# A decoder trunk in split fp32: the gates' first product on paired token factors, weight sums begun a step earlier, and loads issued by the blocks in use

## The chip, the core and the metric

The kernel runs on one core of a Trainium2 chip. A core has five engines with a queue of instructions each: TensorE (PE in the profile; its weight loads are PEld), VectorE (DVE), ScalarE (ACT), GpSimd (POOL) and SyncE (SP, which here only issues transfers). Sixteen DMA engines carry the transfers that SP and POOL issue. The metric is the device time of one execution in microseconds (us), the median of several runs.

## The reference

Two layers over 512 tokens of 1024 features, all in fp32: a gated short convolution with a gated feed-forward behind it, then windowed attention with 16 heads and a gated feed-forward again. The feed-forwards hold most of the work: `w_gate_up` is 1024 x 5632, `w_down` 2816 x 1024.

```python
D_MODEL, BATCH, SEQ, DEPTH = 1024, 1, 512, 2
D_FF = ((8 * D_MODEL // 3 + 255) // 256) * 256          # 2816

def swiglu(h, w_gate_up, w_down):
    g, u = jnp.split(h @ w_gate_up, 2, axis=-1)
    return (jax.nn.silu(g) * u) @ w_down

def reference(x, ...):
    h = x
    for l in range(DEPTH):
        if l < N_A:
            mix = short_conv_mixer(rmsnorm(h, a_pre_norm[l]), a_w_in[l], a_conv_w[l], a_w_out[l])
            h = h + rmsnorm(mix, a_post_norm[l])
        else:
            ...
            attn = sliding_window_sink_attention(q, k_sh, v_sh, b_sinks[j]) @ b_w_o[j]
            h = h + rmsnorm(attn, b_post_norm[j])
        ff = swiglu(rmsnorm(h, ffn_pre_norm[l]), ffn_w_gate_up[l], ffn_w_down[l])
        h = h + rmsnorm(ff, ffn_post_norm[l])
    return h
```

## The kernel before

**Split numbers.** Every factor of a product is split into a high part (`whi`, `xhi`: a copy by ScalarE in the type that TensorE multiplies fast) and a low part (`wlo`, `xlo`: the rest, by a subtraction on VectorE), and `mm3` (L190 to L193) multiplies three times: high by low, high by high, low by high.

**Seven products.** The gates (`gate_jobs`, L976) work on one *quarter* at a time: a stretch of `w_gate_up` for 256 gate features and their 256 up features, in ten quarters a layer, 20 in all. Weights and tokens are cut in two halves each way, and a quarter is computed by seven products of half size instead of eight, in the order 1, 2, 6, 5, 7, 3, 4. Each product takes sums of weight blocks (`a11`, `a21`, `s1`, ...) and sums of token tiles. Products 1, 2 and 3 take token tiles as they are (`xhi`, `xlo`: product 1 the first four of eight, 2 and 3 the last four). For products 4 to 7, `factors` (L364) makes sums of tiles, and lays high and low part of each side by side in one wide buffer (`xt`), so that `factors[p][k][2]` is a right-hand side of 512 columns, 256 high and 256 low.

Products 1, 6, 7 and 4 go into the same two banks (`gx`, chain "X"). In `run` (L1032), a product with such a pair and chain "X" is *wide*: eight matmuls of 128x512 multiply the high weights by high and low tokens at once (L1047), the low tokens' sum landing in the bank's second half, and eight of 128x256 add low weights by high tokens to the first half (L1050). All other products use `mm3`: 24 matmuls of 128x256. What is read after a product is in `take` (L1001): ScalarE copies the first half of a bank into `st` (L1024), and VectorE adds the second half (L1008), except after product 1, which has nothing there.

```python
nc.scalar.activation(ste, a, AF.Copy)
if p != 1:
    add(ste, b, ste)
```

**Loads, splits and their order.** The order on each engine is the order in which the code is written (a manual schedule). `in_line` (L474) runs the products as jobs: after a job's matmuls and reads, it writes the splits of the weights of the job three later (`LINE_LEAD`, L469 and L470), then issues on SP the loads (L440) for which a raw buffer comes free, of which there are `N_RAW` = 7, then one late piece of other work. Buffers come from pools in rotation: 43 of 128x512 (`slot`), 14 of 128x1024 (`wide`), four pairs for split weights. A new tile in a buffer waits for the last reader of the old one.

**Sums of weights in memory.** Some of the sums of weight blocks are made by transfers that GpSimd issues (`Sums`, L509): a first step copies blocks into `hsum` in the chip's memory, a second accumulates other blocks onto them, and where four sums are made, two more steps accumulate sums onto sums. At each named place of the program (`c0`, `0f1`, `0p2`, `0s1`: layer, then quarter or down stage) `sum_on` (L558) begins the group that the table `BEGIN` names for it and takes the next step of every group begun before. The transfers are issued a few at a time behind the split of a weight block (`issue`, L529).

**The down stages** (`down_jobs`, L1081) multiply the activations of finished quarters by `w_down` in the same way with seven products, between the quarters. **The attention** (ahead of the second feed-forward) takes the heads in turn; per head scores, maxima, exponents, normalising (`s`, `se`, `rd`), turned and split probabilities (`phi`, `plo`, `lp`, L1374), weighing (`po`), in an order written in a string.

Of the kernel before, what the change touches and what calls it, by code (L numbers as in the profile page):

```python
# [18 lines left out]
S = 512  # L19
# [8 lines left out]

BEGIN = {
# [4 lines left out]
}  # L34


# [15 lines left out]
    "L": "low", "W": "weigh", "O": "out", "Q": "project", "R": "rotate", "H": "split",  # L52
    "G": "weights", "Z": "project", "z": "out",
}
N_SLOT, N_WIDE, N_RAW, N_W = 43, 14, 7, 4
EARLY = 4
HD = 64
NH = 16
# [14 lines left out]
def yoco_kernel(  # L73
# [165 lines left out]
    class Update:  # L239
# [3 lines left out]
        def __init__(self, mix, gain, gpres):  # L243
            self.mix, self.gpres, self.gain = mix, gpres, gain
            self.s, self.v, self.r = (
                small.tile([P, n], F32, tag=tag, name=name(tag))
                for tag, n in (("us", 12), ("uv", 8), ("ur", 8))
            )
            self.x = [[None] * KT for _ in gpres]
            self.xn, self.banks, self.parts = {}, {}, {}  # L250
            self.leaves = False

        def load(self, queue=nc.sync):
# [82 lines left out]
                                        ident)  # L336

        def split(self, n, f, hf):
            if self.x[n][f] is None:
                self.x[n][f] = (slot("xhi", F32R), slot("xlo", F32R))  # L340
            hi, lo = self.x[n][f]
            c = slice(hf * 256, (hf + 1) * 256)
            src = self.banks[f % 4, hf][:, (f // 4) * 256 : (f // 4 + 1) * 256]
            nc.scalar.activation(hi[:, c], src, AF.Copy, scale=g(self.gpres[n], f))
            nc.vector.scalar_tensor_tensor(
                out=lo[:, c], in0=src, scalar=g(self.gpres[n], f), in1=hi[:, c].bitcast(F32),
                op0=ALU.mult, op1=ALU.subtract,
            )
# [15 lines left out]
        def factors(self):  # L364


            x = self.x[0]
            made = {p: [] for p in range(1, 8)}
            for p, k0, c in ((1, 0, 0), (2, 4, 0), (3, 4, 256)):
                made[p] = [[a[:, c : c + 256] for a in x[k0 + k]] for k in range(4)]  # L370
            for j in range(2):
                q11, q21, q12, q22 = (self.parts[i, hf, j] for hf in range(2) for i in range(2))

                nc.vector.tensor_tensor(out=q11, in0=q11, in1=q12, op=ALU.subtract)
                nc.vector.tensor_tensor(out=q12, in0=q22, in1=q12, op=ALU.subtract)
                nc.vector.scalar_tensor_tensor(out=q22, in0=q22, scalar=-1.0, in1=q11,
                                               op0=ALU.mult, op1=ALU.subtract)
                nc.vector.scalar_tensor_tensor(out=q21, in0=q22, scalar=-1.0, in1=q21,
                                               op0=ALU.mult, op1=ALU.subtract)
                for p, q in ((6, q22), (5, q11), (7, q12), (4, q21)):  # L380
                    two = wide("xt", F32R)
                    hi, lo = two[:, :S], two[:, S:]
                    two = two.rearrange("p (i c) -> p i c", i=2)
                    nc.scalar.activation(hi, q, AF.Copy)
                    nc.vector.tensor_tensor(out=lo, in0=q, in1=hi.bitcast(F32),
                                            op=ALU.subtract)
                    made[p] += [[hi[:, c : c + 256], lo[:, c : c + 256], two[:, :, c : c + 256]]
                                for c in (0, 256)]
            return made
# [84 lines left out]
    def in_line(jobs, late, paced=True):  # L474

        raws = []
        for j, job in enumerate(jobs):
            for raw in job.raws:
                if raw not in raws:
                    raws.append(raw)  # L480
                raw.last = j
        n = [0]

        def prepare(j):

            if 0 <= j < len(jobs):
                jobs[j].prepare()
            while n[0] < len(raws) and (n[0] < N_RAW or raws[n[0] - N_RAW].last <= j):
                raws[n[0]].fetch()
                n[0] += 1  # L490
            if j + 1 < len(jobs):
                jobs[j + 1].add()

        for j in range(-1, LINE_LEAD):
            prepare(j)
        late = late()
        for j, job in enumerate(jobs):
            if job.run:
                job.run(job)
            prepare(j + LINE_LEAD)  # L500
            if paced and j + LINE_LEAD < len(jobs):
                issue(1 + len(issues) // 6, jobs[j + LINE_LEAD].begun)
            for _ in range(1 if paced else max(len(late) - 1, 1)):
                if late and not job.alone:
                    late.pop(0)()
            late += job.then() or [] if job.then else []
# [135 lines left out]
        return product  # L642


    xs = [(slot("xhi", F32R), slot("xlo", F32R)) for _ in range(KT)]
    rows = slot("rrow")
    cols = small.tile([P, 4], F32, tag="cols", name=name("cols"))
    ws = [[wsp.tile([P, D], F32R, tag=tag, name=name(tag)) for tag in ("whi", "wlo")]
# [306 lines left out]
    def ffn(l, before, ahead, gain, gpres, following):  # L955
# [20 lines left out]
        def gate_jobs(q, factors, out, to, then):  # L976
# [24 lines left out]
            def take(p):  # L1001
                x, y, z = (banks.get(c) for c in "XYZ")
                st, u, gr = kept
                g0, g1 = (gr.rearrange("p (e h c) -> p e h c", e=2, h=2)[:, :, h]
                          for h in range(2))

                def add(out, a, b):
                    nc.vector.tensor_tensor(out=out, in0=a, in1=b, op=ALU.add)  # L1008

                if p == 2:  # L1010
                    add(g0, tiles(y), tiles(st))
                elif p == 5:
                    nc.scalar.activation(u, z, AF.Copy)
                elif p == 3:
                    add(g1, tiles(z), tiles(st))
                else:
                    for e in range(2):
                        a, b = x[e][:, :256], x[e][:, 256:]
                        ste, ue = (v[:, e * 256 : (e + 1) * 256] for v in (st, u))
                        if p == 7:  # L1020
                            add(ue, a, ue)
                            add(ue, b, ue)
                            continue
                        nc.scalar.activation(ste, a, AF.Copy)  # L1024
                        if p != 1:
                            add(ste, b, ste)
                if p == 4:
                    for g, m in ((g0, st), (g1, u)):
                        nc.vector.scalar_tensor_tensor(out=g, in0=tiles(m), scalar=-1.0, in1=g,
                                                       op0=ALU.mult, op1=ALU.mult)  # L1030

            def run(p):  # L1032
                def products(job):
# [8 lines left out]
                    steps = [(e, k, slice(e * S + k * P, e * S + (k + 1) * P))  # L1042
                             for e in range(2) for k in range(4)]
                    kw = {"skip_group_check": True}
                    if c == "X" and len(factors[p][0]) == 3:
                        for e, k, kk in steps:
                            nc.tensor.matmul(banks[c][e], whi[:, kk], factors[p][k][2],  # L1047
                                             start=opened and k == 0, stop=False, **kw)
                        for e, k, kk in steps:
                            nc.tensor.matmul(banks[c][e][:, :256], wlo[:, kk], factors[p][k][0],  # L1050
                                             start=False, stop=k == 3 and p == 4, **kw)
                    else:
                        for e, k, kk in steps:
                            out = (banks[c][e][:, :256] if c == "X"
                                   else banks[c][:, e * 256 : (e + 1) * 256])
                            mm3(out, whi[:, kk], wlo[:, kk], *factors[p][k][:2],
                                opened and k == 0 and (c == "X" or e == 0),
                                e == 1 and k == 3 and p in (2, 3), **kw)
                    take(p)
                return products  # L1060
# [181 lines left out]
        eng.tensor_tensor(out=a, in0=a, in1=sh, op=ALU.add)  # L1242
        return a

    def rope_split(a, eng):
        hi, lo = slot("rhi", F32R), slot("rlo", F32R)
        nc.scalar.activation(hi, a, AF.Copy)
        eng.tensor_tensor(out=lo, in0=a, in1=hi.bitcast(F32), op=ALU.subtract)
        return hi, lo


    class Queries:
# [16 lines left out]
            self.rot = rope(self.ps, eng)  # L1269

        def split(self, eng=nc.gpsimd):
            self.hi, self.lo = rope_split(self.rot, eng)

    class Heads:

# [111 lines left out]
                    skip_group_check=True)  # L1387

        def out(self):
            hi, lo = slot("ohi", F32R), slot("olo", F32R)  # L1390
            nc.scalar.activation(hi, self.po, AF.Copy)
            nc.vector.tensor_tensor(out=lo, in0=self.po, in1=hi.bitcast(F32), op=ALU.subtract)
            at.append((hi, lo))
# [224 lines left out]
```

## Time and profile before

| | |
|---|---|
| median of three runs | 1024.08 us (1023.93 to 1025.08) |
| profiled execution | 1026.6 us, its span 1024.8 us |
| granted TensorE clock | 0.998 |
| PE busy | 1013.6 us, 99% |
| DVE busy | 857.8 us, 84% |
| ACT busy | 580.7 us, 57% |
| POOL busy | 196.7 us, 19% |
| chain that ended last | PE 80%, DVE 11%, DMA 4% |

The span is the time from the first to the last instruction on the core in the one profiled execution; what lies around it belongs to the execution's own time. A line of a group gives busy time and mean duration in ns, then the idle time of its engine just ahead of it and who ended it. Matmuls overlap, so that a mean duration isn't the time that a matmul takes from the next. A table by stage gives, for each stretch, busy time and number of instructions of each engine, the granted clock, the DMA engines' share and the rate.

### The profile page before, as it was taken

To read this page: it belongs to the slowest core of one execution; us is meant where nothing else is said; L and a number is where in the kernel's file an instruction comes from. 1 tells how busy PE (TensorE), PEld (TensorE's weight loads), DVE (VectorE), ACT (ScalarE), POOL (GpSimd) and SP (SyncE) were. 2 spreads that over 40 slices of the span, in tenths; PEclk is the share of its full clock that TensorE was granted. 3 is DMA by queue.
4 is the path that set the end of the run, shared out by engine and by line. 5 is a ranking of instruction groups with operands and counts; after the bars stand their busy time and mean duration, and the time that the engine had idled before them with its cause. 6 is when DMAs were issued, how large, how long until landed. Compare 5 with 4: busy or idle time off the path is not lost.

```text
span 1024.8 us, 16537 instructions
## 1 busy us (share of the span) xinstructions
PE 1013.6 (99%) x6168; PEld 901.8 (88%) x6168; DVE 857.8 (84%) x1440; ACT 580.7 (57%) x1035; POOL 196.7 (19%) x259
## 2 busy tenths in 40 slices
PE   9999999999999999999999999999999999999997
PEld 8888888999899898898898888889998998989986
DVE  5766768889789988988869998778997898889896
ACT  7222445875655454566476776667666554645641
POOL 0443033112111111000122653232111010100001
PEclk9999999999999999999999999999999999999999
DMA  9897789459979699778504889976899576998742
GB/s 356 287 255 232 187 254 348 140 169 281 344 249 299 195 302 318 256 215 303 182 1 152 199 234 281 246 260 156 262 289 333 169 247 228 299 294 245 242 150 82
DMA packets 66576, 244.52 MB, mean 239 GB/s; under 512 B 7872, under 2 KB 8384, under 8 KB 54720
## 3 DMA queue, kind: packets, MB, share of 16 engines
q1 hardware_dynamic: 51328, 145.98, 38.9%
q0 software_dynamic: 14592, 96.48, 37.2%
q8 instruction: 48, 0.79, 0.3%
q10 hardware_dynamic: 576, 1.02, 0.3%
q14 instruction: 32, 0.26, 0.1%
HBM read 237.15 MB, written 102.76 MB: 332 GB/s over the span
## 4 chain that ended last, share of the span: by engine, by line
PE 80%; DVE 11%; DMA 4%; ACT 2%; issue 2%; POOL 0%; DVEq 0%; ACTq 0%
PE gx L1047 10%; PE gx L1050 5%; DMA raw<-in_w_gb_dram 4%; PE pcub L193 4%; PE pcub L191 4%; PE pcub L192 4%; PE gz L193 3%; PE gz L192 3%; PE gz L191 3%; PE px L191 3%; PE px L192 3%; PE px L193 3%; PE pmix L192 2%; PE pmix L191 2%; PE pmix L193 2%
## 5 line engine op out<-in xcount | busy, mean ns | idle before, releaser
L470 DVE TENSOR_TENSOR wlo<-raw,whi 128x1024 fp32r<-128x1024 f32 x225 | 274.6, 1227 | 65.6 <-ACT whi L469 65.6
L469 ACT ACTIVATE whi<-raw 128x1024 fp32r<-128x1024 f32 x225 | 233.8, 1051 | 108.3 <-DVE raw L457 25.0
L1047 PE MATMUL gx<-xt,whi 128*128 128x512 f32 x480 | 120.4, 393 | 0.7 <-DVE st L1008 0.7
L1047 PEld LDWEIGHTS gx<-xt,whi 128*128 128x128 f32 x480 | 86.3, 189 | 16.6 <-DVE st L1008 1.2
L538 POOL DMA_DIRECT2D hsum<-in_w_gb_dram x96 | 63.4, 747 | 141.4 <-ACT whi L469 82.3
L1024 ACT ACTIVATE st<-gx 128x256 f32<-128x256 f32 x120 | 42.7, 379 | 60.8 <-PE gx L1050 36.4
L538 POOL DMA_DIRECT2D hsum<-hsum x32 | 25.2, 789 | 260.1 <-ACT whi L469 208.2
L1050 PEld LDWEIGHTS gx<-xt,wlo 128*128 128x128 f32 x480 | 65.5, 190 | 4.7
L1050 PE MATMUL gx<-xt,wlo 128*128 128x256 f32 x480 | 66.9, 282 | 0.0
L1008 DVE TENSOR_TENSOR st<-gx,st 128x256 f32<-128x256 f32 x160 | 62.8, 420 | 3.4 <-ACT st L1024 1.6
L192 PE MATMUL pcub<-xhi,whi 128*128 128x512 f32 x168 | 65.4, 389 | 0.0
L191 PE MATMUL pcub<-xlo,whi 128*128 128x512 f32 x168 | 65.4, 389 | 0.0
L193 PE MATMUL pcub<-xhi,wlo 128*128 128x512 f32 x168 | 65.4, 389 | 0.0
L1063 ACT ACTIVATE gr<-gr 128x1024 f32<-128x1024 f32 x20 | 21.3, 1063 | 50.6 <-DVE gr L1008 50.6
L191 PE MATMUL px<-wlo,ahi 128*128 128x512 f32 x120 | 46.8, 390 | 0.1
L192 PE MATMUL px<-whi,ahi 128*128 128x512 f32 x120 | 46.7, 389 | 0.0
L193 PE MATMUL px<-whi,alo 128*128 128x512 f32 x120 | 46.7, 389 | 0.0
L193 PE MATMUL gx<-xhi,wlo 128*128 128x256 f32 x160 | 45.4, 284 | 0.8 <-DVE wlo L470 0.8
L193 PE MATMUL gz<-xhi,wlo 128*128 128x256 f32 x160 | 45.5, 284 | 0.0
L191 PE MATMUL gx<-xlo,whi 128*128 128x256 f32 x160 | 45.4, 283 | 0.0
L191 PE MATMUL gy<-xlo,whi 128*128 128x256 f32 x160 | 45.3, 283 | 0.0
L192 PE MATMUL gy<-xhi,whi 128*128 128x256 f32 x160 | 45.3, 283 | 0.0
(265 smaller groups left out, 3062.8 us busy)
## 6 DMA issues: line engine op xcount, KB each, us to landing
hsum<-in_w_gb_dram POOLq DMA_DIRECT2D x96, 512.0 KB, 7.8
raw<-hsum SPq DMA_DIRECT2D x88, 512.0 KB, 7.9
raw<-in_w_gb_dram SPq DMA_DIRECT2D x60, 512.0 KB, 7.7
hsum<-in_w_dn_dram POOLq DMA_DIRECT2D x36, 512.0 KB, 9.1
raw<-in_w_dn_dram SPq DMA_DIRECT2D x32, 512.0 KB, 6.1
hsum<-hsum POOLq DMA_DIRECT2D x28, 512.0 KB, 6.7
raw<-in_w_in_dram SPq DMA_DIRECT2D x21, 512.0 KB, 8.1
hsum<-in_w_dn_dram POOLq DMA_DIRECT2D x12, 768.0 KB, 12.2
```

What stands on the lines that cost most here:

```text
L191: nc.tensor.matmul(out, whi, xlo, start=start, stop=False, **kw)
L192: nc.tensor.matmul(out, whi, xhi, start=False, stop=False, **kw)
L193: nc.tensor.matmul(out, wlo, xhi, start=False, stop=stop, **kw)
L469: self.begun = nc.scalar.activation(hi[:, :n], raw, AF.Copy)
L470: nc.vector.tensor_tensor(out=lo[:, :n], in0=raw, in1=hi[:, :n].bitcast(F32), op=ALU.subtract)
L538: nc.gpsimd.dma_start(dst, src, max_dma_last_dim=4 * 4 * S, **kw))
L1008: nc.vector.tensor_tensor(out=out, in0=a, in1=b, op=ALU.add)
L1024: nc.scalar.activation(ste, a, AF.Copy)
L1047: nc.tensor.matmul(banks[c][e], whi[:, kk], factors[p][k][2], start=opened and k == 0, stop=False, **kw)
L1050: nc.tensor.matmul(banks[c][e][:, :256], wlo[:, kk], factors[p][k][0], start=False, stop=k == 3 and p == 4, **kw)
L1063: nc.scalar.activation(kept[2], kept[2], AF.Silu)
```

## The change

- **Side by side.** The tiles of the first four of eight token factors (`BOTH` = 4) are made in wide buffers with high and low part side by side. Product 1 of every quarter becomes a wide product, and after it VectorE adds the second half of each bank to `st`, as after the others.
- **Buffers.** `N_SLOT` goes from 43 to 35 and `N_WIDE` from 14 to 18. The convolution's first token factors, the split heads of the attention (`rhl`) and part of its output (`ohl`) move from two small buffers into one wide one.
- **Sums.** The table `BEGIN` begins six groups of layer 0 and three of layer 1 one place earlier.
- **Loads.** `in_line` issues a load when fewer than seven blocks fetched so far are still needed after the current job, instead of when the block seven places back is done with.

```diff
 BEGIN = {
     "c0": "g00", "c1": "g01", "c3": "g02", "c4": "d00", "c6": "g03", "o0": "g04", "o1": "d01",
-    "0f1": "g05", "0p0": "g06", "0p1": "d02", "0p2": "g07", "0p3": "g08", "0s1": "g09", "0p5": "d03",
+    "0f0": "g05", "0f1": "g06", "0p0": "d02", "0p1": "g07", "0p2": "g08", "0p4": "g09", "0p5": "d03",
     "a0": "g10", "a1": "g11", "a3": "g12", "a4": "d10", "a6": "g13", "a7": "g14", "a8": "d11",
-    "1f0": "g15", "1f1": "g16", "1p0": "d12", "1p2": "g17", "1p3": "g18", "1s1": "g19", "1p5": "d13",
+    "1f0": "g15", "1f1": "g16", "1p0": "d12", "1p1": "g17", "1p2": "g18", "1p4": "g19", "1p5": "d13",
 }
...
-N_SLOT, N_WIDE, N_RAW, N_W = 43, 14, 7, 4
+N_SLOT, N_WIDE, N_RAW, N_W = 35, 18, 7, 4
+BOTH = 4
...
         def split(self, n, f, hf):
+            if self.x[n][f] is None and n == 0 and f < BOTH:
+                two = wide("xhl", F32R)
+                self.x[n][f] = two[:, :S], two[:, S:]
+                self.both[f] = two.rearrange("p (i c) -> p i c", i=2)
...
-                made[p] = [[a[:, c : c + 256] for a in x[k0 + k]] for k in range(4)]
+                made[p] = [[a[:, c : c + 256] for a in x[k0 + k]]
+                           + [two[:, :, c : c + 256] for two in self.both[k0 + k :][:1] if two]
+                           for k in range(4)]
...
-            while n[0] < len(raws) and (n[0] < N_RAW or raws[n[0] - N_RAW].last <= j):
+            while n[0] < len(raws) and sum(raw.last > j for raw in raws[:n[0]]) < N_RAW:
                 raws[n[0]].fetch()
                 n[0] += 1
...
                         nc.scalar.activation(ste, a, AF.Copy)
-                        if p != 1:
-                            add(ste, b, ste)
+                        add(ste, b, ste)
...
-                    if c == "X" and len(factors[p][0]) == 3:
+                    if c == "X":
                         for e, k, kk in steps:
                             nc.tensor.matmul(banks[c][e], whi[:, kk], factors[p][k][2],
                                              start=opened and k == 0, stop=False, **kw)
...
         def split(self, eng=nc.gpsimd):
-            self.hi, self.lo = rope_split(self.rot, eng)
+            self.hi, self.lo = rope_split(self.rot, eng, True)
...
         def out(self):
-            hi, lo = slot("ohi", F32R), slot("olo", F32R)
+            if self.t < BOTH:
+                hi, lo = halves("ohl", F32R)
+            else:
+                hi, lo = slot("ohi", F32R), slot("olo", F32R)
```

VectorE, in the second quarter of layer 0, around the reads after its product 1 (`wlo` is the low split of a weight block, `st` takes the reads of the banks `gx`). Before:

```order
L1029 SCALAR_TENSOR_TENSOR gr_2022<-st_2021,gr_2022 128x2x256
L470 TENSOR_TENSOR wlo_2246<-raw_2000,whi_2245 128x1024
L470 TENSOR_TENSOR wlo_2284<-raw_2008,whi_2283 128x1024
L581 TENSOR_TENSOR a_456_2251<-gr_2022,a_456_2251 128x256
L1008 TENSOR_TENSOR gr_2254<-gy_2291,st_2252 128x2x256
L470 TENSOR_TENSOR wlo_2318<-raw_2055,whi_2317 128x1024
```

And now:

```order
L1037 SCALAR_TENSOR_TENSOR gr_2016<-st_2015,gr_2016 128x2x256
L478 TENSOR_TENSOR wlo_2238<-raw_1992,whi_2237 128x1024
L1017 TENSOR_TENSOR st_2244<-gx_2247,st_2244 128x256
L1017 TENSOR_TENSOR st_2244<-gx_2248,st_2244 128x256
L478 TENSOR_TENSOR wlo_2270<-raw_2000,whi_2269 128x1024
L589 TENSOR_TENSOR a_448_2243<-gr_2016,a_448_2243 128x256
L1017 TENSOR_TENSOR gr_2246<-gy_2279,st_2244 128x2x256
L478 TENSOR_TENSOR wlo_2306<-raw_2043,whi_2305 128x1024
```

Two reads of the banks stand between the two splits, ahead of what followed there.

GpSimd's queue, at the sums of the last quarters and of the last down stage of layer 0 (`hsum_152` to `155` and `156` to `159` are two groups of a quarter each, `hsum_172` to `175` the last down stage's). Before:

```order
L538 DMA hsum_155<-in_w_gb_dram 64x2048
L538 DMA hsum_152<-in_w_gb_dram 64x2048
L538 DMA hsum_153<-in_w_gb_dram 64x2048
L538 DMA hsum_154<-hsum_152 64x2048
L538 DMA hsum_156<-in_w_gb_dram 64x2048
L538 DMA hsum_157<-in_w_gb_dram 64x2048
L538 DMA hsum_158<-in_w_gb_dram 64x2048
L538 DMA hsum_159<-in_w_gb_dram 64x2048
L538 DMA hsum_155<-hsum_154 64x2048
L538 DMA hsum_156<-in_w_gb_dram 64x2048
L538 DMA hsum_157<-in_w_gb_dram 64x2048
L538 DMA hsum_172<-in_w_dn_dram 64x2048
```

And now:

```order
L546 DMA hsum_152<-in_w_gb_dram 64x2048
L546 DMA hsum_153<-in_w_gb_dram 64x2048
L546 DMA hsum_154<-hsum_152 64x2048
L546 DMA hsum_155<-hsum_154 64x2048
L546 DMA hsum_156<-in_w_gb_dram 64x2048
L546 DMA hsum_157<-in_w_gb_dram 64x2048
L546 DMA hsum_158<-in_w_gb_dram 64x2048
L546 DMA hsum_159<-in_w_gb_dram 64x2048
L546 DMA hsum_156<-in_w_gb_dram 64x2048
L546 DMA hsum_157<-in_w_gb_dram 64x2048
L546 DMA hsum_158<-hsum_156 64x2048
L546 DMA hsum_172<-in_w_dn_dram 64x2048
```

The first group's last sum no longer stands behind the second's first copies, and the second's third sum is issued ahead of the down stage's.

VectorE, in the attention, at the low split of a head's turned probabilities, with the engines that each instruction waits for. Before:

```order
L1240 TENSOR_TENSOR ra_6140<-pk_5285,ctab_5288 128x512
L1374 TENSOR_TENSOR plo_6083<-pt_6077,phi_6082 128x512 [waits Activation_49,Pool_49]
L1374 TENSOR_TENSOR lp_5620<-pt_6084,lp_5619 128x2x128 [waits Activation_49]
L1340 TENSOR_TENSOR se_6108<-se_6108,rs_6109 128x4
L1342 RECIPROCAL rd_6158<-se_6108 128x4 [waits DVE_49]
```

And now:

```order
L1246 TENSOR_TENSOR ra_6063<-pk_5213,ctab_5216 128x512 [waits DVE_49,PE_49]
L1380 TENSOR_TENSOR plo_6007<-pt_6001,phi_6006 128x512 [waits DVE_49,PE_49,Activation_49]
L1380 TENSOR_TENSOR lp_5548<-pt_6008,lp_5547 128x2x128 [waits Activation_49]
L1346 TENSOR_TENSOR se_6032<-se_6032,rs_6033 128x4
L1348 RECIPROCAL rd_6081<-se_6032 128x4 [waits DVE_49]
```

The order is the same; `plo` now also waits for TensorE, whose product read the buffer that it takes over.

More of the change, by code (lines that the diff above doesn't have):

```diff
@@ L250, in __init__ @@
             self.xn, self.banks, self.parts = {}, {}, {}
+            self.both = [None] * KT
             self.leaves = False
@@ L642, in seven @@
         return product
-    xs = [(slot("xhi", F32R), slot("xlo", F32R)) for _ in range(KT)]
+    xs = [halves("xhl", F32R) if k < BOTH else (slot("xhi", F32R), slot("xlo", F32R))
+          for k in range(KT)]
     rows = slot("rrow")
@@ L1053, in products @@
                         for e, k, kk in steps:
[L1054 to L1057, printed above, removed]
+                            mm3(banks[c][:, e * 256 : (e + 1) * 256], whi[:, kk], wlo[:, kk],
+                                *factors[p][k][:2], opened and e == k == 0,
                                 e == 1 and k == 3 and p in (2, 3), **kw)
@@ L1243, in rope, with rope_split @@
         return a
-    def rope_split(a, eng):
-        hi, lo = slot("rhi", F32R), slot("rlo", F32R)
+    def rope_split(a, eng, large=False):
+        hi, lo = halves("rhl", F32R) if large else (slot("rhi", F32R), slot("rlo", F32R))
         nc.scalar.activation(hi, a, AF.Copy)
```

## The prediction

> **What bounds the kernel now.** I read the page first: which engine is never idle, and which groups the change touches.
>
> ```profile
> span 1024.8 us, 16537 instructions
> PE 1013.6 (99%) x6168; PEld 901.8 (88%) x6168; DVE 857.8 (84%) x1440; ACT 580.7 (57%) x1035; POOL 196.7 (19%) x259
> ...
> L470 DVE TENSOR_TENSOR wlo<-raw,whi 128x1024 fp32r<-128x1024 f32 x225 | 274.6, 1227 | 65.6 <-ACT whi L469 65.6
> ...
> L1047 PE MATMUL gx<-xt,whi 128*128 128x512 f32 x480 | 120.4, 393 | 0.7 <-DVE st L1008 0.7
> ...
> L1008 DVE TENSOR_TENSOR st<-gx,st 128x256 f32<-128x256 f32 x160 | 62.8, 420 | 3.4 <-ACT st L1024 1.6
> ...
> L193 PE MATMUL gx<-xhi,wlo 128*128 128x256 f32 x160 | 45.4, 284 | 0.8 <-DVE wlo L470 0.8
> ```
>
> TensorE is the bound (99%); a change can win only by fewer TensorE streams, or out of the 11 us in which it waits. The tempting figure is the mean duration: 284 ns for a 128x256 product, 393 for a 128x512. But matmuls overlap, so next the timeline of TensorE, where the distance between two starts is what a matmul costs (columns: start, duration in us).
>
> ```profile
> 204.25 0.28 PE L191 MATMUL gx<-xlo,whi 128*128 128x256 f32 x1
> 204.37 0.28 PE L192 MATMUL gx<-xhi,whi 128*128 128x256 f32 x1
> 204.49 0.28 PE L193 MATMUL gx<-xhi,wlo 128*128 128x256 f32 x1
> ...
> 210.01 2.00 PE L1047 MATMUL gx<-xt,whi 128*128 128x512 f32 x8
> 211.85 1.12 PE L1050 MATMUL gx<-xt,wlo 128*128 128x256 f32 x8
> 212.80 0.28 PE L191 MATMUL gz<-xt,whi 128*128 128x256 f32 x1
> ```
>
> A 128x256 product comes every 0.12 us; eight wide ones take 211.85 - 210.01 = 1.84 us (0.23 each), and the eight narrow ones behind them 0.95. Then a table by stage: stretches that are one gates quarter each (19.90 us when undisturbed), or a down stage (263.95, 391.19, 896.59).
>
> ```profile
> core 0: us, PE busy (x) PEld busy (x) DVE busy (x) ACT busy (x) POOL busy (x), PEclk, DMA share, GB/s
> 204.25:224.15 19.90, 19.90 (x147) 18.89 (x146) 17.27 (x27) 14.24 (x22) 1.83 (x3) 1.00 0.63 212
> 224.15:244.05 19.90, 19.90 (x147) 18.90 (x146) 19.21 (x30) 12.35 (x20) 4.47 (x7) 1.00 0.71 199
> 244.05:263.95 19.90, 19.90 (x147) 18.90 (x146) 19.21 (x30) 12.35 (x20) 3.66 (x6) 1.00 1.00 323
> 263.95:292.53 28.58, 28.58 (x128) 23.65 (x127) 21.57 (x30) 16.79 (x24) 3.41 (x5) 1.00 1.00 344
> 371.29:391.19 19.90, 19.90 (x147) 18.89 (x146) 17.35 (x28) 12.23 (x20) 4.47 (x7) 1.00 0.91 252
> 391.19:410.35 19.16, 19.16 (x86) 15.59 (x85) 14.51 (x22) 6.83 (x9) 2.36 (x3) 1.00 1.02 323
> 410.35:431.91 21.56, 20.53 (x146) 19.11 (x146) 21.18 (x30) 12.28 (x18) 1.56 (x2) 1.00 0.78 254
> 896.59:915.65 19.06, 19.06 (x86) 15.77 (x85) 17.00 (x24) 6.83 (x9) 2.38 (x3) 1.00 1.02 315
> 915.65:936.28 20.63, 20.16 (x145) 18.93 (x144) 18.86 (x27) 12.27 (x18) 1.55 (x2) 1.00 0.81 263
> ```
>
> Two quarters are longer than 19.90: that at 410.35 by 1.66 us and that at 915.65 by 0.73. Ahead of both, the 16 DMA engines are fully taken (1.02). The chain of waits and the waits around the first one say why.
>
> ```profile
> 389.06 20.07 DMA raw<-in_w_gb_dram
> ...
> 410.38 1.10 issue
> ```
>
> ```profile
> ACT whi L469 <- DMA raw<-hsum: 6.9, 2, 3.9
> ACT whi L469 <- DMA raw<-in_w_gb_dram: 4.0, 1, 4.0
> ```
>
> ```profile
> PE gx L193 <- DVE wlo L470: 0.8, 1, 0.8
> PE gx L1047 <- DVE st L1008: 0.3, 1, 0.3
> ```
>
> One weight load took 20.07 us, ScalarE waited for three loads between 385 and 412, and TensorE stood still behind the late split and then behind VectorE, which catches up for 21.18 of 21.56 us.
>
> **The product side by side.** Each of 20 quarters loses 24 x 0.12 = 2.88 us and gains 1.84 + 0.95 = 2.79 us: -0.09 (0.087 with the starts unrounded), -1.74 us in all. The mean durations would give 24 x 284 - 8 x 393 - 8 x 284 = 1.4 us a quarter, 28 us in all; the starts exclude that.
>
> [...]
>
> What it adds: the second half of each bank now holds a sum of its own, so VectorE gets two more 128x256 adds a quarter (0.42 us each, 0.75 for the pair in the rows below), 40 in all. They stand between two splits of weights, ahead of the next wide product, which may not open the bank before they have read it; and ScalarE's first copy comes later, as a bank is now full only near the product's end. In 16 quarters VectorE has 2 us or more of idle time, or hides the pair in time that comes free with the late loads (below), so nothing is added. In four (224.15, 244.05 and their twins in layer 1) it has 0.69 us, and the rows show what lies behind it:
>
> ```profile
> 227.98 2.35 DVE L470 TENSOR_TENSOR wlo<-raw,whi 128x1024 fp32r<-128x1024 f32 x2
> ...
> 234.25 0.75 DVE L1008 TENSOR_TENSOR st<-gx,st 128x256 f32<-128x256 f32 x2
> ...
> 237.36 1.23 DVE L470 TENSOR_TENSOR wlo<-raw,whi 128x1024 fp32r<-128x1024 f32 x1 [0.55 <-ACT whi L469]
> ```
>
> The adds go in between the two splits of the first row, end about 229.1 + 0.75 = 229.86, and the second wide product wants to start at 229.82 (229.91 before, less 0.09): with the hand-over about 0.1 late. Everything behind moves by 0.67 (the pair's pitch), so that the adds that ended at 235.00 end at 235.67, against a third wide product at 235.5 to 235.6: another 0.15. The gap of 0.55 then swallows the rest. About 0.25 us in each of the four, +0.98 in all; the ends are 0 and the whole pair, 4 x 0.75 = 3.0. Gates together: -1.74 + 0.98 = -0.76.
>
> **Sums begun sooner.** SP's loads keep their order, and each waits for the same split that frees its buffer, so the rule "by blocks in use" moves nothing that binds. What moves is GpSimd's queue: the running sums of six weight groups in layer 0 and three in layer 1 start a step earlier. Between 371.29 and 410.35 ten transfers become eight (six accumulations become four).
>
> ```profile
> q0 software_dynamic: 838, 5.42, 54.6%
> q1 hardware_dynamic: 2473, 5.74, 41.2%
> ```
>
> These ten (q0) take 54.6% of 39.06 us, 2.1 us each of all 16 engines; two accumulations, which read and write, I put at 5 us (4.3 at that mean). The late loads then land some 5 us sooner. ScalarE's longest wait for them was 4.0 us and TensorE's stall is a quarter of that, so the stalls should go: 1.66 + 0.73 + 0.09 (the down stage at 391.19 against 19.07 undisturbed) = -2.48. The ends: 0 and -2.48. I take the whole, since 5 us is more than the longest wait. Late next is nothing there: the first product now also wants its low weights only 1.84 us into the product.
>
> In exchange more lie between 204 and 292: four more in the first quarter above, where the DMA share is 0.63 (the second has 0.71), one fewer in the third, three more in the down stage at 263.95. That is six more, 12.6 us at 2.1 each; the first two quarters have 0.37 x 19.9 + 0.29 x 19.9 = 13 us idle for them. But the down stage has a share of 1.00 already, and its three come too late for that idle time: 6.3 us at the mean, of which I expect its early loads, issued ahead of the last of the three, to see about half. The load that counts is split here, for a product at 292.53:
>
> ```profile
> 286.01 1.06 ACT L469 ACTIVATE whi<-raw 128x1024 fp32r<-128x1024 f32 x1 [2.16 <-DVE s L585]
> ```
>
> 292.53 - 286.01 - 1.06 = 5.5 us of lead (the low split fits into the product's first 1.84). So +0.1 us for the rest, ends 0 and 7.1 (second rival).
>
> **Buffers.** There are 35 small buffers for 43 and 18 wide ones for 14. Of the new waits that this makes one binds, in the attention: a low split of probabilities (`plo`) now takes a buffer that the weighing product (`po`) of the head before it still reads.
>
> ```profile
> 579.93 0.68 DVE L1374 TENSOR_TENSOR plo<-pt,phi 128x512 fp32r<-128x512 f32 x1
> 580.53 0.42 DVE L1374 TENSOR_TENSOR lp<-pt,lp 128x256 fp32r<-128x256 f32 x1
> 580.86 1.07 DVE L1340 TENSOR_TENSOR se<-se,rs 128x4 f32<-128x4 f32 x1
> ```
>
> ```profile
> 580.42 0.28 PE L191 MATMUL po<-plo,vt 128*128 128x256 f32 x1
> ...
> 581.01 0.28 PE L193 MATMUL po<-phi,vt 128*128 128x256 f32 x1
> ...
> 585.49 0.59 PE L1357 MATMUL pt<-ident,s 128*128 128x128 f32 x3 [0.44 <-DVE s L1345]
> ```
>
> The split started at 579.93 and must now wait until that product's reads end, at about 581.3: 1.4 us. Queued behind it on VectorE are `lp`, `se` and the normalising `s`, for which TensorE already waits 0.44 us at 585.49. VectorE has no idle time to make it up (18.72 busy of the 19.00 us from 580), so I take +1.4. The ends: +0.3 (`se` takes 1.07 us for four columns in that place, and could be short elsewhere) and +2.
>
> **Sum**: -0.76 - 2.48 + 0.1 + 1.4 = -1.7 us. The profiled execution has a span of 1024.8 (1026.6 with what lies around it); its changed twin would have 1023.1. From the median of 1024.08: **1022.4 us**. A measurement of this kernel can tell about 0.2%, or 2.05 us, from no change (1022.0 and 1026.1), so this is "same", close to the edge.
>
> **Rivals.**
> - The attention's wait is hidden, because `se` shrinks by what the wait takes and because TensorE's later waits there overlap it: -0.76 - 2.48 + 0.1 + 0.2 = -2.9, 1021.1 us. For: `se` at 1.07 us. Against: TensorE is already behind VectorE at 585.49. Or the four tight quarters swallow their adds: -1.7 - 0.98 = -2.7, 1021.4. Together 0.36.
> - Slower: the down stage at 263.95 passes the whole backlog on. Its share is 1.00 and that of the quarter ahead too; if the 12.6 us of added transfers found no idle time before it, the load split at 286.01 comes 12.6 us later, and its product 12.6 - 5.5 = 7.1 us late: -1.7 + 7.1 = +5.4, 1029.5. It costs from 5.5 us of lateness on, and decides from 5.5 + 1.7 = 7.2 on. Against: the 13 us of idle DMA before it. 0.13. [...]
> - The earlier sums don't cure the late loads, as these wait for something else: -0.76 + 0.1 + 1.4 = +0.7, 1024.8. Against: ScalarE's waits name DMA. 0.09.
> - The mean durations were right: 996 us. 0.01.
>
> **How the numbers follow.** The forecast has 0.41. Faster by over 0.2%: 0.36 + 0.01 = 0.37. Within 0.2%: 0.41 + 0.09 = 0.50. Slower: 0.13. The range reaches from 1020.0 (all gains, and half of the tight quarters' and attention's prices saved) to 1026.0; it leaves out the slower rival and little on the other side.
>
> **What would show it.** Right: quarters of 19.81 us, those at 410 and 915 too; the tight ones near 20.06, with TensorE waiting for VectorE's `st` ahead of a wide product; ScalarE's waits for DMA near 400 and 905 nearly gone; VectorE waiting for TensorE at `plo` near 580 by 1.4 us. Wrong: TensorE waiting at 292 for weights, quarters of 20.4 or more throughout (the pair fully exposed), or still over 20.5 us at 410.

## The result, and the profile after

The changed kernel takes 1028.96 us (median of 5 runs, 1028.36 to 1030.02) against 1024.08 (1023.62 to 1026.02): a ratio of 1.0046, 95% interval 1.0034 to 1.0057, so about 4.7 us slower. That is above the predicted range (1020.0 to 1026.0) and is the case that had 0.13. The profiled execution took 1028.36 us, its span is 1026.6.

The page of the changed kernel, the lines that answer to those shown of before:

```profile
span 1026.6 us, 16268 instructions
PE 1013.1 (99%) x6008; PEld 893.6 (87%) x6008; DVE 869.5 (85%) x1480; ACT 581.8 (57%) x1035; POOL 196.8 (19%) x259
...
L1017 DVE TENSOR_TENSOR st<-gx,st 128x256 f32<-128x256 f32 x200 | 78.0, 420 | 2.6 <-ACT st L1033 0.5
...
L192 PE MATMUL px<-wlo,ahi 128*128 128x512 f32 x120 | 47.8, 398 | 3.2 <-DVE mix L647 3.0
```

160 products are gone and 40 adds have come, as planned. New is the last line: TensorE waits 3.2 us ahead of a product of the down stages (`px`), and that product's mean has grown from 390 to 398 ns. The table by stage of the changed kernel (four gates quarters and, last two, the first down stage of each layer):

```profile
core 0: us, PE busy (x) PEld busy (x) DVE busy (x) ACT busy (x) POOL busy (x), PEclk, DMA share, GB/s
223.57:243.38 19.81, 19.81 (x138) 18.47 (x137) 19.67 (x32) 12.35 (x20) 4.48 (x7) 1.00 1.00 309
243.38:263.31 19.93, 19.93 (x138) 18.52 (x137) 19.79 (x32) 12.39 (x20) 3.41 (x5) 1.00 1.02 310
413.38:433.18 19.80, 19.80 (x138) 18.48 (x137) 18.05 (x28) 11.67 (x17) 0.77 (x1) 1.00 0.57 179
918.38:938.20 19.82, 19.82 (x138) 18.50 (x137) 18.07 (x28) 11.69 (x17) 0.77 (x1) 1.00 0.58 175
...
263.31:296.05 32.74, 30.49 (x129) 24.72 (x127) 22.41 (x31) 16.88 (x24) 5.26 (x8) 0.95 1.02 336
771.02:800.72 29.70, 28.90 (x128) 23.58 (x127) 19.98 (x28) 15.98 (x23) 5.26 (x8) 1.00 1.03 338
```

Most quarters take the 19.81 us that were forecast, those that had waited for late loads too. Of the tight ones, forecast at 20.06, the second of each layer takes 19.81 and the third 19.93 and 19.92. The loss is in the first down stages: 32.74 and 29.70 us for 28.58 before, with the DMA engines full and eight transfers of GpSimd in each for five and four. How it comes about in layer 0 is seen in the waits of that stage, in the chain, and in the timelines of ScalarE, VectorE and TensorE:

```profile
ACT whi L477 <- DMA raw<-hsum: 6.1, 2, 4.4
```

```profile
268.50 18.95 DMA raw<-hsum
```

```profile
287.55 0.63 ACT L477 ACTIVATE whi<-raw 128x512 fp32r<-128x512 f32 x1 [1.77 <-DMA raw<-hsum]
```

```profile
288.21 0.69 DVE L478 TENSOR_TENSOR wlo<-raw,whi 128x512 fp32r<-128x512 f32 x1 [0.38 <-ACT whi L477]
...
289.49 1.28 DVE L647 TENSOR_TENSOR mix<-mix,px 128x512 f32<-128x512 f32 x2
```

```profile
287.59 0.39 PE L194 MATMUL py<-whi,alo 128*128 128x512 f32 x1
290.23 0.50 PE L192 MATMUL px<-wlo,ahi 128*128 128x512 f32 x1 [2.25 <-DVE mix L647]
...
291.03 0.62 PE L192 MATMUL px<-wlo,ahi 128*128 128x512 f32 x1
291.45 0.63 PE L193 MATMUL px<-whi,ahi 128*128 128x512 f32 x1
```

A load of a sum took 18.95 us; in the trace of before the same load took 13.32. Its split on ScalarE waits for it, the low split on VectorE behind that, and behind the low split, in VectorE's order, the add `mix` that frees the bank of the next `px`. TensorE doesn't wait for the weights that come late, but for an add that is queued behind their split. In the same place before, that split and that add stood at 283.21 and 286.61 (ScalarE and VectorE), both behind TensorE and not behind a load:

```profile
283.21 0.63 ACT L469 ACTIVATE whi<-raw 128x512 fp32r<-128x512 f32 x1 [1.28 <-PE px L193]
```

```profile
286.61 1.37 DVE L639 TENSOR_TENSOR mix<-mix,px 128x512 f32<-128x512 f32 x2 [0.69 <-PE px L193]
```

From 287.59 to 290.23 TensorE's starts are 2.64 us apart where 0.23 is usual, a stall of 2.4 us, but the stage lost 4.15. (Stalls below are counted in the same way, as the time beyond the usual distance.) The rest is in the last lines: from 291.03 on eight matmuls start 0.43 us apart, not 0.23, and the granted clock is low there (columns as in the table):

```profile
288.00:290.30 2.30, 0.07 (x1) 0.07 (x1) 2.08 (x5) 0.40 (x2) 0.00 (x0) 1.00 1.04 305
290.30:294.40 4.10, 4.10 (x11) 3.22 (x12) 4.10 (x6) 2.93 (x4) 0.00 (x0) 0.59 0.98 386
```

For 3.4 us (291.03 to 294.44) TensorE runs at a granted clock of 0.50; from the stall's end on it loses another 1.7 us. In layer 1 the stall is 0.96 us and no slow matmuls follow (granted clock 1.00).

In the attention, VectorE waits for `plo` as forecast, 1.26 us. TensorE waits twice behind it, at `pt`, for 0.7 us in all, where before it waited once for 0.44; a product `po` ahead of that comes 0.28 us late (the waits of VectorE and of TensorE from 562 and 575 us on):

```profile
DVE plo L1380 <- ACT se L1341: 1.3, 1, 1.3
```

```profile
PE pt L1363 <- DVE s L1351: 0.7, 2, 0.4
```

VectorE's wait is named after ScalarE's `se`, but that had been done for 0.5 us; by the order of instructions it is the one for TensorE's `po`.

### The profile page after: what moved, and what is told of

Its sections match the earlier page's. It is cut to its first block, busy times and chain, and to the rows that moved or that the text cites. A ratio compares the mean times of both kernels' runs of the same rounds, so it can differ in the third digit from the quotient of the medians.

```text
span 1026.6 us, 16268 instructions
## 1 busy us (share of the span) xinstructions
PE 1013.1 (99%) x6008; PEld 893.6 (87%) x6008; DVE 869.5 (85%) x1480; ACT 581.8 (57%) x1035; POOL 196.8 (19%) x259
## 3 DMA queue, kind: packets, MB, share of 16 engines
q0 software_dynamic: 14592, 96.48, 36.7%
q10 hardware_dynamic: 576, 1.02, 0.3%
## 4 chain that ended last, share of the span: by engine, by line
PE 84%; DVE 7%; DMA 4%; ACT 3%; issue 2%; POOL 0%; DVEq 0%; SPq 0%; ACTq 0%
PE gx L1055 13%; PE gx L1058 7%; PE pcub L193 4%; PE pcub L192 4%; PE pcub L194 4%; PE gz L194 4%; PE gz L193 4%; PE gz L192 4%; PE px L192 3%; PE px L193 3%; PE px L194 3%; PE pmix L192 2%; PE pmix L193 2%; PE pmix L194 2%; DMA raw<-in_w_gb_dram 2%; DMA raw<-hsum 2%
## 5 line engine op out<-in xcount | busy, mean ns | idle before, releaser
L1017 DVE TENSOR_TENSOR st<-gx,st 128x256 f32<-128x256 f32 x200 | 78.0, 420 | 2.6 <-ACT st L1033 0.5
L192 PE MATMUL gz<-xt,whi 128*128 128x256 f32 x160 | 45.3, 283 | 0.0
L193 PE MATMUL gz<-xt,whi 128*128 128x256 f32 x160 | 45.3, 283 | 0.0
L194 PE MATMUL gy<-xhi,wlo 128*128 128x256 f32 x160 | 45.3, 283 | 0.0
L194 PE MATMUL gz<-xt,wlo 128*128 128x256 f32 x160 | 45.3, 283 | 0.0
L192 PE MATMUL gz<-xlo,whi 128*128 128x256 f32 x160 | 45.3, 283 | 0.0
```

Of the source, the lines that this page charges most:

```text
L192: nc.tensor.matmul(out, whi, xlo, start=start, stop=False, **kw)
L193: nc.tensor.matmul(out, whi, xhi, start=False, stop=False, **kw)
L194: nc.tensor.matmul(out, wlo, xhi, start=False, stop=stop, **kw)
```

## The experiments

All experiments are compared with the kernel before on the same chip. "Old table" and "new table" are the two versions of `BEGIN`. "The second profile of before" is that of `before_again`. The attention's stretch runs from the end of layer 0's quarters to the start of layer 1's. Diffs of `BEGIN` from `four_copies` on show only the entries that change, out of longer lines.

**The kernel before once more** (`before_again`; no edit).

> The kernel before once more, for a second profile of it. Its profiled execution took 1026.6 us where its median is 1024.1. Theory: the 2.4 us of stalls by late loads in the quarters at 410 and 915 us belong to that execution; a second profile has a span nearer to 1022 and quarters there nearer to 19.9 us. Rival: the stalls are in every execution and the 2.5 us lie elsewhere; then 21.6 and 20.6 us again.

Measured: 1024.09 us (1023.57 to 1026.86), a profiled execution of 1023.98 with a span of 1022.2. Its two quarters:

```profile
409.92:429.82 19.90, 19.90 (x146) 18.89 (x145) 19.03 (x27) 11.55 (x17) 1.56 (x2) 1.00 0.82 276
913.55:933.67 20.12, 20.12 (x146) 18.95 (x145) 18.87 (x27) 12.29 (x18) 1.54 (x2) 1.00 0.84 274
```

19.90 and 20.12 us instead of 21.56 and 20.63: the two spans differ by 2.6 us, and 2.3 of it are these stalls and the down stage ahead of the first. What I had taken for a cost of the kernel is a cost of some of its executions. ScalarE's waits for late loads are as long as in the first profile, though:

```profile
ACT whi L469 <- DMA raw<-hsum: 5.7, 2, 3.0
ACT whi L469 <- DMA raw<-in_w_gb_dram: 4.7, 1, 4.7
```

So these loads are late in this execution too, and only just in time for TensorE.

**The new table alone** (`sums_only`), in the kernel before:

```diff
-    "0f1": "g05", "0p0": "g06", "0p1": "d02", "0p2": "g07", "0p3": "g08", "0s1": "g09", "0p5": "d03",
+    "0f0": "g05", "0f1": "g06", "0p0": "d02", "0p1": "g07", "0p2": "g08", "0p4": "g09", "0p5": "d03",
...
-    "1f0": "g15", "1f1": "g16", "1p0": "d12", "1p2": "g17", "1p3": "g18", "1s1": "g19", "1p5": "d13",
+    "1f0": "g15", "1f1": "g16", "1p0": "d12", "1p1": "g17", "1p2": "g18", "1p4": "g19", "1p5": "d13",
```

> The kernel before with the new table of the sums alone. Theory (the sums begun sooner fill the DMA engines in the first down stage of each layer): slower by 4 to 5.5 us, with TensorE waiting near 288 us for 2 us or more and near 794 for about 1. Rival (the adds after the first product delay VectorE's splits, and so the loads): within 1 us of before.

Measured: 1031.06 us (1029.16 to 1032.84), ratio 1.0061 (1.0048 to 1.0075). The first down stages:

```profile
264.00:293.28 29.28, 28.90 (x129) 23.57 (x127) 20.05 (x28) 15.79 (x23) 5.25 (x8) 1.00 1.03 338
768.26:803.70 35.44, 31.04 (x128) 25.16 (x127) 22.83 (x31) 16.71 (x24) 5.23 (x8) 0.90 0.96 322
```

The table alone makes the whole loss and more. Which layer pays differs: here layer 1 has the long stall (4.56 us, and 2.3 us by slow matmuls behind it, at a granted clock of 0.50), while layer 0 gets off with 0.69.

**The old table in the changed kernel** (`old_sums`): the same lines the other way round.

> The changed kernel with the old table of the sums. Theory: the first down stages take 28.6 us again, the gates gain 1.7 us, the attention loses 0.75: about 1.0 us faster than before (1023.1). Rival (adds and buffers delay the loads): still 4 us slower than before.

Measured: 1024.85 us (1023.12 to 1026.25), ratio 1.0002 (0.9993 to 1.0011). The first down stages take 28.59 us each again, the quarters 19.81 (the third of each layer 19.90), and the stretch with the attention is 0.72 us longer than in the second profile of before. The forecast 1023.1 came out only in some executions: in the profiled one (1025.46) the quarters at 410 and 914 are late once more, by 0.53 and 1.15 us over the second profile of before. With the old table these quarters are not always just in time; whether the two adds have a part in it is looked at next.

**A narrow first product with the changed buffers** (`narrow_first`): the old table, and

```diff
-                        add(ste, b, ste)
+                        if p != 1:
+                            add(ste, b, ste)
...
-                    if c == "X":
+                    if c == "X" and p != 1:
```

with `mm3` for product 1 as before.

> The changed kernel with the old table of the sums and the first product with 24 matmuls of 128x256 as before (no added reads); buffers and loads stay changed. Theory: the side-by-side product is worth its 0.087 us a quarter and its adds cost nothing but a later VectorE in the quarters at 410 and 914, so quarters are 19.90 us again, and the attention still loses 0.7: +0.7 on the kernel before, 1024.8 to 1025.3. Rival (the adds hold TensorE up): faster than the kernel with the old table and the wide product, by 0.5 us or more.

Measured: 1025.21 us (1024.35 to 1026.01), ratio 1.0012 (1.0003 to 1.0021). The quarters are 19.90 us again, and the attention's stretch is 0.71 longer than before. In the attention the buffers alone thus cost all that was lost there. Against the wide product this is 0.4 us slower by the medians and 1.0 by the ratios, with intervals that overlap. In both profiled executions, with the adds and without, the quarter at 410 was late by the same 0.53 us over the second profile of before; that at 914 was late only with them, in one execution of each. So the adds are not shown to have made these quarters late.

**Only the four copies moved back** (`four_copies`), one group of four sums a layer begun at the end of the first down stage:

```diff
-    "0p1": "g07", "0p2": "g08", "0p4": "g09"
+    "0p1": "g07", "0s0": "g08", "0p4": "g09"
...
-    "1p1": "g17", "1p2": "g18", "1p4": "g19"
+    "1p1": "g17", "1s0": "g18", "1p4": "g19"
```

> The changed kernel with one group of each layer (g08, g18: four copies and four accumulations) begun at the end of the first down stage; all other sums stay early. Theory: the four copies that the change puts into the first down stage, on DMA engines that are full there, make its loads late; without them the stage takes at most 29.2 us in layer 0 and 28.6 in layer 1, and the kernel is 1022.8 to 1024.5. Rival (the sums begun sooner ahead of it fill the engines): the stage still takes 31 us or more in layer 0, 1027 or more.

Measured: 1023.20 us (1022.77 to 1025.16), ratio 0.9995 (0.9986 to 1.0004). The stage in layer 0:

```profile
263.50:293.21 29.71, 28.89 (x129) 23.57 (x128) 20.73 (x29) 16.90 (x24) 3.13 (x4) 1.00 0.97 315
```

29.71 us there and 28.59 in layer 1, with four transfers of GpSimd in each instead of eight. By one profiled execution of each kernel, these four copies make 3 of the 4.15 us in layer 0 and all of the 1.11 in layer 1; the other 1.1 in layer 0 (29.71 us, over the 29.2 expected) are left to the groups begun sooner ahead of it.

The traces of all these kernels bear the wait for the load out. The load that was late above is issued 5.1 to 5.2 us into the stage in each of them. Where it lands up to 20.8 us into the stage (`past_stage`, below), the stage keeps its 28.59 us; at 21.0 to 22.7 it loses 0.7 to 1.1 us; at 24.1, in layer 0 of the changed kernel, 4.15, and at 24.9, in layer 1 of `sums_only`, 6.85. Why the load lands later in one layer here and in the other there isn't shown.

**Sums sooner, but past that stage** (`past_stage`, in the changed kernel; `past_alone`, the same table in the kernel before). Against the old table:

```diff
-    "0p2": "g07", "0p3": "g08", "0s1": "g09"
+    "0p2": "g07", "0s0": "g08", "0p4": "g09"
...
-    "1p2": "g17", "1p3": "g18", "1s1": "g19"
+    "1p2": "g17", "1s0": "g18", "1p4": "g19"
```

> The changed kernel with only the sums of the last two quarters' groups begun sooner, and these only after the first down stage (g08 at its end, g09 a step earlier; layer 1 alike). Theory: no stall in the first down stages, and the loads ahead of 410 and 915 us land earlier than with the old table: 1022.5 to 1023.5. Rival (any sum begun sooner costs): 1025 or more.

> The kernel before with the table of the kernel past_stage alone (no wide first product, no changed buffers). Theory: 0 to 0.5 us faster than before (only late loads in the quarters at 410 and 914 go, which differ between executions): 1023.6 to 1024.3, and slower than past_stage by about 1 us (1.74 gained there, 0.7 lost). Rival (the table makes the whole gain of past_stage): 1023.1.

Measured: `past_stage` 1023.09 us (1022.48 to 1024.00), ratio 0.9986 (0.9977 to 0.9995); `past_alone` 1023.97 (1023.41 to 1025.01), ratio 0.9997 (0.9988 to 1.0006). With the table that leaves the first down stage alone, both stages take 28.59 us in both kernels, and the quarters at 410 and 914 have the length of the others (19.81 in `past_stage`, 19.90 in `past_alone`). The 11 executions of `past_stage` lie within 1.5 us of each other, where 27 of the kernel before spread over 2.5. The side-by-side product is what sets the two apart: in the profiles the gates are 1.71 us shorter with it and the attention 0.8 longer with its buffers, and the medians differ by 0.9 (the intervals of the two ratios overlap).

**The rule for loads alone** (`loads_only`), in the kernel before:

```diff
-            while n[0] < len(raws) and (n[0] < N_RAW or raws[n[0] - N_RAW].last <= j):
+            while n[0] < len(raws) and sum(raw.last > j for raw in raws[:n[0]]) < N_RAW:
```

> The kernel before with the rule for loads alone (by blocks in use). Theory: each load waits for the same release of a buffer, so nothing that binds moves: 1023.7 to 1024.7, stages of the same length. Rival (loads go out sooner and fill the DMA engines in the first down stage): 1025 or more, with the first down stages longer than 28.6 us.

Measured: 1024.57 us (1023.66 to 1025.71), ratio 0.9998 (0.9989 to 1.0007). The first down stages and the quarters have the lengths of the second profile of before, but for 0.09 us at 913: the rule does nothing that can be measured.

**The attention's wait** (`past_swap`: `past_stage` with two neighbours exchanged in the order; `swap36`: that with one small buffer more).

```diff
-    "... E10 E11 Z1 z0 K W0 L2 L3 A A A N0 W1 W2 N1 W3 g1 z1"
+    "... E10 E11 Z1 z0 K W0 L3 L2 A A A N0 W1 W2 N1 W3 g1 z1"
```

```diff
-N_SLOT, N_WIDE, N_RAW, N_W = 35, 18, 7, 4
+N_SLOT, N_WIDE, N_RAW, N_W = 36, 18, 7, 4
...
-    ones = const.tile([P, P], F32, name="ones")
-    nc.vector.memset(ones, 1.0)
     ones_r = const.tile([P, P], F32R, name="ones_r")
     nc.vector.memset(ones_r.bitcast(F32), 1.0)
+    ones = ones_r.bitcast(F32)
```

> The kernel past_stage with the two low splits of probabilities that stand next to each other in the attention exchanged, so that the one that waits for no product of TensorE goes first and fills 0.35 us of VectorE's wait. Theory (VectorE's wait at the low split is what the attention loses, 0.7 us): the stretch that holds the attention gets 0.3 us shorter, 1022.6 to 1023.0. Rival (the loss comes from GpSimd or another buffer): no change within 0.1 us in that stretch.

> The kernel past_swap with one small buffer more (36; the space comes from keeping one matrix of ones instead of two). Theory: the low split then waits for a matmul two places earlier, 0.24 us less: 1022.4 to 1023.0, and the attention's stretch 0.5 us shorter than in past_stage. Rival: as past_swap.

Measured: `past_swap` 1022.08 us (1021.64 to 1023.59), ratio 0.9975 (0.9965 to 0.9985); `swap36` 1021.97 (1021.66 to 1022.49), ratio 0.9973 (0.9963 to 0.9983). The exchange won 1.15 us in the attention's stretch, not 0.3; the buffer more is within the noise. VectorE in `past_swap`:

```profile
577.95 0.41 DVE L1380 TENSOR_TENSOR lp<-pt,lp 128x256 fp32r<-128x256 f32 x1
579.24 0.69 DVE L1380 TENSOR_TENSOR plo<-pt,phi 128x512 fp32r<-128x512 f32 x1 [0.88 <-PE po L194]
579.85 0.15 DVE L1346 TENSOR_TENSOR se<-se,rs 128x4 f32<-128x4 f32 x1
```

The wait is 0.88 for 1.26 us, as meant, and is now named after `po`. The other 0.8 us come from `se`, which took 0.95 us in that place in `past_stage` (1.07 before) and takes 0.15 here. Both kernels beat the kernel before, by 2.6 and 2.8 us by the ratios, and the changed one; between the two nothing is shown.

**The clock behind a stall** (`stalls` and `stalls_many`: the kernel before, with ScalarE's copies after product 1 repeated, so that the next wide product waits for the bank).

```diff
-                        nc.scalar.activation(ste, a, AF.Copy)
+                        again = {(0, 4): 9, (1, 4): 12}.get((l, q), 0) if p == 1 else 0
+                        for _ in range(1 + again):
+                            nc.scalar.activation(ste, a, AF.Copy)
```

In `stalls_many` the line is `again = 9 if p == 1 and q else 0`.

> The kernel before with ScalarE's copies after the first product repeated in the fifth quarter: nine more pairs in layer 0, twelve more in layer 1, so that the next wide product waits for the bank, about 1.1 us in layer 0 and about 3 in layer 1. Theory (a stall of TensorE over some 2 us is followed by about 10 matmuls at half speed): the matmuls behind the first stall come every 0.23 us, those behind the second every 0.43 for about 4 us, with a granted clock well under 1.00 there. Rival (the slow matmuls in the changed kernel come from the full DMA engines or the late operands): full speed behind both.

> The kernel before with ScalarE's copies repeated nine times in 18 quarters (all but the first of each layer), which stops TensorE for about 3 us in each. [...] Rival (the length alone decides, and what came before the 2.4 us stall of the changed kernel differed): all 18 alike.

Measured: one execution each, 1038.59 and 1137.57 us. In `stalls` the first stall was 3.00 us long (not 1.1), with full speed behind it (granted clock 1.00); the second 4.24, just after one of 1.31, with 2.5 us lost by slow matmuls (granted clock 0.50 in the first 3.3 us behind it). This alone told little, since the longer one also had another ahead of it; `stalls_many`, with many stalls of 3.00 us, shows whether the length alone decides. Two of them, the stall and the 4 us behind it:

```profile
384.04:387.30 3.26, 0.43 (x3) 0.04 (x1) 0.00 (x0) 3.04 (x9) 0.00 (x0) 0.97 0.00 0
387.30:391.30 4.00, 4.00 (x18) 3.61 (x19) 3.11 (x4) 2.84 (x5) 1.30 (x2) 0.60 0.40 61
409.02:412.30 3.28, 0.45 (x3) 0.06 (x1) 0.00 (x0) 3.06 (x9) 0.00 (x0) 1.00 0.09 31
412.30:416.30 4.00, 4.00 (x29) 3.80 (x30) 3.12 (x4) 2.97 (x6) 2.43 (x3) 1.00 0.44 61
```

The same work and the same stall: once a granted clock of 0.60 and 18 matmuls in 4 us, once 1.00 and 29. Of nine stalls of 3.00 us that had no other just ahead of them (eight here, one in `stalls`), seven were followed by 1.4 to 2.8 us of loss at a lower clock (against the same matmuls in the second profile of before), and two by no more than 0.2 in the next 30 matmuls. The DMA engines were nearly idle in the two stalls shown (shares of 0.00 and 0.09) and far from full behind them (0.40 and 0.44), so here the low clock came without full DMA engines.

## Why the prediction was wrong

The sum was -1.7 us; measured on the medians it is +4.9, and on the two profiled executions that hold no stall of before's (the changed one against the second profile of before) +4.4. Step by step:

- **The product side by side, -1.74: right.** A quarter that nothing else holds up went from 19.90 to 19.81 us; the starts, not the mean durations, gave the price.
- **The four tight quarters, +0.98: too much.** Measured is nothing in the second quarters and 0.12 and 0.11 in the third ones, though VectorE is busy 19.67 of 19.81 us in the first of them, 0.14 us from full. One more place came, in the quarter behind layer 1's first down stage: at 806 us a wide product starts 0.22 us late, behind VectorE's `st`, and the quarter takes 20.11 us, 0.32 more than its twin in layer 0. My working put one quarter's 0.67 us on the next two products by hand and left almost no slack; most of it was there.
- **Stalls by late loads, -2.48: wrong, since they are not in the median.** I took two stalls of one profiled execution for a property of the kernel, though it took 1026.6 us and the median is 1024.08. The working named that difference only at its end, where the sum was moved over to the median as it was. The second profile shows 0.22 us (at 913) left to win, and the changed kernel won that. That the sums begun sooner make those loads land earlier was right: ScalarE's waits for DMA there (12.3 us from 385 to 412 and 12.4 from 890 to 920 in the first profile of before) are gone in the changed kernel.
- **The first down stage, +0.1: the term that failed.** Measured +4.15 in layer 0 and +1.11 in layer 1, which I had not priced. Two things went wrong in it. The lead was that of the wrong load: I took the first block of the next quarter (5.5 us), while the load that decides is one of the stage's own, which is split at 283.21 and has an add behind its low split that a bank waits for. In the rows of before that add had 0.69 us of VectorE's idle time and about 1.1 us at the bank, and the load 0.9 ahead of its split: 2.7 us in all, against loads that came over 5 us later. And a stall was priced as its length; the matmuls at the low clock behind it added 1.7 us. The second rival had the mechanism, late loads in this stage, but waited for the wrong load and carried the same wrong lead. That its 1029.5 us lie near the measured 1028.96 is partly luck: it put 7.1 us into layer 0 and none into layer 1, and took 2.48 off for the late loads.
- **Loads against GpSimd's queue, for the slower rival.** It assumed that the loads bear the delay when GpSimd's queue is filled; how the DMA engines divide their time between the two queues isn't shown. What was measured agrees with it: in the changed kernel's stage 743 packets of GpSimd's queue took 50.6% of the DMA engines and 2431 of the loads' queue 51.5%, where it had been 437 with 36.7% and 2796 with 63.1%, and the load took 18.95 us for 13.32.
- **Buffers, +1.4: right in mechanism, half in size.** VectorE's wait was 1.26 us, TensorE lost 0.7: +0.28 at `po` and +0.44 at `pt`. The lower end, +0.3, was for a shorter `se`; in the changed kernel it still took 0.97 us, and only the exchange brought it to 0.15.
- **Loads by blocks in use, 0: right**, by a run of its own.

The terms as measured, -1.74 for the product, +0.23 and +0.32 for the adds, -0.22 at 913, +5.26 for the first down stages and +0.7 for the attention, make +4.6, within 0.2 of the +4.4 between the two profiles.

## What to carry to other kernels

In this kernel's first down stages the DMA engines were full (shares of 1.02 and 1.03), and the transfers moved ahead were paid by the loads queued there (18.95 us for 13.32); where that can happen, ask which load has the least lead to the bound engine, and follow each split to everything that stands behind it in its engine's order, not only to the product that reads it. A stall seen in one profiled execution is a gain only if other executions have it, so set the profile's own time against the median before anything is built on its stalls. And a change of several parts is best taken apart: here one part won 1.7 us, and a table that had nothing to do with it lost three times as much.

## What the runs showed of the hardware

- A stop of TensorE of 2.4 us was followed by eight matmuls at half speed (granted clock 0.50), at 0.43 us for 512 columns; stops of 3.00 us were followed by a loss of 1.4 to 2.8 us or by next to none, and one of 2.54 (in `stalls_many`, at 300 us) by next to none. A stop of 0.96 us cost 0.15 beyond itself, at a granted clock of 1.00. So the length of a stop alone didn't decide in these runs; what did isn't shown.
- A sum of four columns on VectorE (`se`) took 0.95 to 1.07 us behind one instruction and 0.15 behind another. Why isn't settled.
